# A decoder block on one core: three norms' weights loaded first, the memory's later, seven unread products ahead of them

## The chip, the cores and the metric

The kernel runs on one core of one Trainium2 chip. The metric is device time in microseconds (us) of one execution. TensorE (PE, with its weight loads listed apart as PEld), VectorE (DVE), ScalarE (ACT), GpSimd (POOL) and SyncE (SP) each take their own instructions in a fixed order and wait for each other, and for DMA transfers, through semaphores. ACTq and SPq are DMA issues from the ACT and the SP stream.

## What is computed

One layer (DEPTH is 1) of a decoder block on a 256x2048 input, all in float32. What matters here is its start: the first norm and the first projection.

```
def rmsnorm(x, gain):
    y = xf * lax.rsqrt(jnp.mean(xf * xf, axis=-1, keepdims=True) + NORM_EPS)
    return (y * gain.astype(jnp.float32)).astype(x.dtype)
...
        h = rmsnorm(x, g[0])
        y = hybrid_mixer(h, ...)                       # z = h @ w_in, then attention, gMLP, RWKV-7
        x = x + rmsnorm(y, g[1])
        h = rmsnorm(x, g[2])
        y = memory_cross_attention(h, rmsnorm(mem, mem_src_gain[l]), ...)
        x = x + rmsnorm(y, g[3])
        h = rmsnorm(x, g[4])
        y = conv_ffn(h, ...)
        x = x + rmsnorm(y, g[5])
```

So four weight vectors of 2048 are needed as columns (one value per partition): g[0], g[2], g[4] and `mem_src_gain`. Only g[0] is needed at the start; `mem_src_gain` is used hundreds of microseconds later.

## The kernel before

All matrix products run on TensorE as sums of three products of "hi" and "lo" halves of float32 values. A weight block of 512 KB is loaded into a `raw` buffer (four of them) from the SP stream; ACT casts it to `hi` (L234) and DVE subtracts to get `lo` (L236), three buffers of each. `wstat` (L255) multiplies them with the transposed input: for every 128 rows of weights one product hi x h.hi (L266), one hi x h.lo (L268) and one lo x h.hi (L271), each 128x256.

The input is loaded by eight transfers `x` (L437, names x_76 to x_92 in the listings), and transposed on TensorE in 128x128 pieces (L389) into PSUM tiles `auxp` and `auxq`. ACT multiplies a piece by the norm's weight, a column of `gpar`, and writes the hi half `h` (L375); DVE writes the lo half (L376). There are 16 such pairs. The norm's row factor is applied later: ACT squares x (L408), the sums go over DVE and POOL (L417) to a product with the unit matrix (L424) that lays the factors out along a row, `rrow`.

`gpar` holds the four norms' weights. Before, two transfers from the ACT stream fill the 64 rows of `grow`, one transpose (L469) and one copy (L470) make `gpar` of it:

```
grow = sp.tile([4 * KT, P], F32, name="grow")                                                   # L452
nc.scalar.dma_start(grow[:3 * KT, :], gains[0:6:2].rearrange("g (k p) -> g k p", p=P))          # L454
nc.scalar.dma_start(grow[3 * KT:, :], a["mem_src_gain"][0].rearrange("(k p) -> k p", p=P))      # L455
...
nc.tensor.transpose(ps[:, :4 * KT], grow, ident[:4 * KT, :4 * KT])                              # L469
gcopy = nc.vector.tensor_copy(gpar, ps[:, :4 * KT])                                             # L470
```

`split` makes every `lo` wait to be issued until after `gcopy`. The first projections are a 128-column block (the low-rank inputs, 48 products into one PSUM tile) and then blocks of 256 columns for the RWKV keys (96 products into two tiles). Small tables follow between them: a product `tab` x `oneh` (L531), transposes of `prow` (L512) and of `crow` (L543). When the 128-column block is finished, DVE and ACT make `zl` of it (L607 to L609), and three times a pair of loads `wa` from the ACT stream (L633, L634, one buffer) feeds eight recorded products with `zl` (L642).

The order of each engine's stream is set when the program is built, by a scheduler: it goes by data dependences, by priorities that the code gives (`high_priority` with an offset, `issue_after`), and by the scheduler's own estimate of when things are ready. Each engine then keeps to that order whatever happens on the chip. So a change to a few lines can move instructions of other lines.

Of the kernel before, what the change touches and what calls it, by code (L numbers as in the profile page):

```python
# [12 lines left out]
F32 = mybir.dt.float32  # L13
# [7 lines left out]
P = 128  # L21
D = 2048
S = 256
KT = D // P
# [148 lines left out]
def hybrid_block(tc, a, out, dbg=None):  # L173
    nc = tc.nc
    dbg = dbg or {}
    with ExitStack() as ctx:
# [14 lines left out]
        def mk(pool, tag, bufs, shape=(P, 512), dt=F32):  # L191
            t = pool.tile(list(shape), dt, tag=tag, bufs=bufs, name=nm(tag))
            return t
# [8 lines left out]
        def auxp():  # L202
            return mk(pp, "auxp", 2)

        def auxq():
            return mk(pp, "auxq", 2)
# [11 lines left out]
        def raw_load(src, k0, nk, c0, nco, ahead=AHEAD):  # L218
            if (k0, nk, c0, nco) in early:
                return early.pop((k0, nk, c0, nco))  # L220
            raw = mk(wp, "raw", RAW_BUFS, (P, RAW))
            rv = raw[:, :nk * nco].rearrange("p (k c) -> p k c", k=nk)
            with tc.high_priority(offset=ahead):
                nc.sync.dma_start(rv, src[k0 * P:(k0 + nk) * P, c0:c0 + nco]
                                  .rearrange("(k p) c -> p k c", p=P))
            return rv
# [185 lines left out]
        def factors_of(part):  # L412
# [4 lines left out]
            last_pow[0] = nc.gpsimd.tensor_tensor(r, ss, mhalf[:, :2], op=ALU.pow)  # L417
            return r

        def over_rows(r):  # L420

            ps = auxp()
            for t in range(2):
                nc.tensor.matmul(ps[:, t * P:(t + 1) * P], lhsT=r[:, t:t + 1].to_broadcast([P, P]), rhs=ident,  # L424
                                 start=True, stop=True)
            row = mk(cp, "rrow", 1, (P, S))
            nc.vector.tensor_copy(row, ps[:, :S])
            return row
# [19 lines left out]
        gains = a["sandwich_gains"][0]  # L448
        x2d = a["x"][0]
        start = ExitStack()  # L450
        sp = start.enter_context(tc.tile_pool(name="sp", bufs=1))
        grow = sp.tile([4 * KT, P], F32, name="grow")  # L452
        with tc.high_priority(offset=4 * AHEAD):
            nc.scalar.dma_start(grow[:3 * KT, :], gains[0:6:2].rearrange("g (k p) -> g k p", p=P))  # L454
            nc.scalar.dma_start(grow[3 * KT:, :], a["mem_src_gain"][0].rearrange("(k p) -> k p", p=P))  # L455

            def first_weights():
                early[0, 8, COL_LO, P] = raw_load(a["w_in"][0], 0, 8, COL_LO, P, 0)
            xt = load_rows(x2d, lambda: mk(sp, "x", 8), nc.sync, first_weights)
# [4 lines left out]
        with tc.high_priority(offset=4 * AHEAD):  # L464
            ident = cp.tile([P, P], F32, name="ident")
            make_identity(nc, ident)
            gpar = cp.tile([P, 4 * KT], F32, name="gpar")
            ps = auxp()
            nc.tensor.transpose(ps[:, :4 * KT], grow, ident[:4 * KT, :4 * KT])  # L469
            gcopy = nc.vector.tensor_copy(gpar, ps[:, :4 * KT])  # L470

        def gcol(n):
            return lambda k: gpar[:, n * KT + k:n * KT + k + 1]
# [1 line left out]
        with tc.high_priority(offset=4 * AHEAD):  # L475
            hT = Packed(2)
            pins = []
            for _ in transposed(hT, xt, gcol(0), hbuf):
                pins.append(hT.last)
        rx = row_factors(xt, lambda: mk(sp, "tmp", 4), (None, None, pins[3], pins[5]))  # L480
        xrow = over_rows(rx)


# [17 lines left out]
        for key, src, n in (("mu", a["rwkv_mu"][0], 21), ("w0", a["rwkv_w0"][0], 6),  # L501
                            ("a0", a["rwkv_a0"][0], 6), ("k_k", a["rwkv_k_k"][0], 6),
                            ("k_a", a["rwkv_k_a"][0], 6),
                            ("r_k", a["rwkv_r_k"][0].rearrange("h d -> (h d)"), 6),
                            ("ag", a["attn_out_gain"][0], 6), ("sg", a["sgu_out_gain"][0], 4),
                            ("sb", a["sgu_b"][0].rearrange("g i -> (g i)"), 8)):
            nc.sync.dma_start(prow[r0:r0 + n, :], src.rearrange("(n p) -> n p", p=P))
            off[key] = r0
            r0 += n
        par = cp.tile([P, NPR], F32, name="par")  # L510
        ps = auxp()
        nc.tensor.transpose(ps[:, :NPR], prow[:NPR, :], ident[:NPR, :NPR])  # L512
        nc.vector.tensor_copy(par, ps[:, :NPR])
        omu = cp.tile([P, 21], F32, name="omu")
# [15 lines left out]
        ps = auxp()  # L530
# [10 lines left out]
        ps = auxp()  # L541
# [18 lines left out]
        def colt():  # L560
            return mk(mp, "col", 8)
# [447 lines left out]
        ps = wstat(w_in, COL_LO, P, hT)  # L1009
# [7 lines left out]
        for key, col, mucol, new in (("K", COL_CK, 6, colt), ("R", COL_CR, 0, colt),  # L1017
                                     ("V", COL_CV, 12, lambda: vt()[:, :512])):
            for i in range(3):
                take("v" if key == "V" else "col")  # L1020
                g = new()
                ps = wstat(w_in, col + i * 256, 2 * P, hT)
# [5 lines left out]
        ps = wstat(w_in, COL_LO + P, 2 * P, hT)  # L1028
# [349 lines left out]
        for j in range(2):  # L1378
            ps = wstat(wkv, j * 256, 256, mT)
            k = colt()  # L1380
# [7 lines left out]
        for j in range(2):  # L1388
            ps = wstat(wq, j * 256, 256, h2T)
# [6 lines left out]
        for h in range(4):  # L1396
            qh = qTs[h // 2][:, (h % 2) * S:(h % 2) * S + S]
            kh = kTs[h // 2][:, (h % 2) * S:(h % 2) * S + S]
            ps = auxq()
            for t in range(2):  # L1400
                nc.tensor.matmul(ps[:, t * S:(t + 1) * S], lhsT=qh[:, t * P:(t + 1) * P], rhs=kh,
                                 start=True, stop=True)
# [31 lines left out]
        for h in range(4):  # L1434
            po = auxq()
            for m in range(2):
                nc.tensor.matmul(po[:, :S], lhsT=vm[m][:, h * P:(h + 1) * P], rhs=pTs[h][:, m * S:(m + 1) * S],
                                 start=(m == 0), stop=(m == 1))
# [95 lines left out]
        for j in range(1, FT // 2):  # L1534
            g = mk(fp, "gv", 4)
            ps = wstat2(w_up, j * 256, 256, h3T)
# [6 lines left out]
            ps = wstat2(w_up, D_FF + j * 256, 256, h3T)  # L1543
# [39 lines left out]
```

## Time and profile before

| | |
|---|---|
| runs | 1348.06, 1348.78, 1353.36 us; median 1348.78 |
| profiled execution | 1352.56 us, its span 1350.8 us |
| mean granted TensorE clock in it | 0.992 |
| PE busy | 98% |
| DVE, ACT, POOL busy | 65%, 52%, 11% |

PE is busy nearly throughout; the slices of the page in which it is not are the first and the last. Idle time of the other engines matters only where PE waits for them. The granted clock is given as a share of full speed: 1.00 is 2.4 GHz, 0.50 is 1.2 GHz.

### The profile page before, as it was taken

Reading aid. Unit: us, or ns where it says so; the run is one execution under the profiler, and the core shown is the slowest. Engines: PE = TensorE matmul, PEld = TensorE weight load, DVE = VectorE, ACT = ScalarE, POOL = GpSimd, SP = SyncE. Lnnn points to the kernel's source line nnn. Section 1 sums busy time; section 2 is a strip of 40 time slices with the busy share of each in tenths; the row PEclk is TensorE's granted clock in tenths of the full one; section 3 lists DMA queues with packets and bytes.
Section 4 is the critical chain, followed back from the end, with each engine's and each line's share of the span. In section 5 each row is a group of like instructions: output and inputs, shape, how many; then the busy total and the mean of one; then the engine's idle time right before and its main releaser. Section 6 shows DMA issues by size and latency. Waiting matters only on the chain.

```text
span 1350.8 us, 20948 instructions
## 1 busy us (share of the span) xinstructions
PE 1317.6 (98%) x8184; PEld 1157.1 (86%) x8184; DVE 873.6 (65%) x1300; ACT 708.3 (52%) x1077; POOL 143.9 (11%) x179
## 2 busy tenths in 40 slices
PE   6899999999999999999999999999999999999997
PEld 6789979998987889879888888888888888888886
DVE  5578974466666666566867677776767674445444
ACT  6665363244456655456655555555555553444442
POOL 3010101120014100000111111111111120000000
PEclk9899999999999999999999999999999999999999
DMA  7444553155447755444666666666666666666553
GB/s 226 138 142 142 156 172 111 40 178 165 141 143 271 251 177 187 156 154 129 195 192 189 188 189 191 193 191 188 188 190 191 193 221 193 196 190 196 191 195 133
DMA packets 189841, 238.82 MB, mean 177 GB/s; under 512 B 7920, under 2 KB 144013, under 8 KB 189741
## 3 DMA queue, kind: packets, MB, share of 16 engines
q1 hardware_dynamic: 185514, 225.23, 53.7%
q0 software_dynamic: 3376, 11.29, 2.5%
q8 instruction: 64, 1.05, 0.3%
q10 hardware_dynamic: 851, 0.95, 0.2%
q14 instruction: 36, 0.29, 0.1%
HBM read 235.33 MB, written 2.12 MB: 176 GB/s over the span
## 4 chain that ended last, share of the span: by engine, by line
PE 93%; DVE 2%; issue 1%; DMA 1%; ACT 1%; POOL 1%; ACTq 0%; DVEq 0%; POOLq 0%
PE mm L302 23%; PE mm L304 11%; PE mm L324 11%; PE mm L326 11%; PE mm L330 11%; PE mm L271 6%; PE mm L266 5%; PE mm L268 5%; PE mm L287 2%; DMA wa<-in_rwkv_w_up_dram 1%; PE auxq L678 1%; DVE lo L236 1%; DMA raw<-in_w_in_dram 0%; PE auxp L389 0%; PE auxq L389 0%
## 5 line engine op out<-in xcount | busy, mean ns | idle before, releaser
L236 DVE TENSOR_TENSOR lo<-raw,hi 128x1024 fp32r<-128x1024 f32 x422 | 519.4, 1232 | 368.4 <-ACT hi L234 365.4
L234 ACT CAST hi<-raw 128x1024 fp32r<-128x1024 f32 x422 | 443.4, 1051 | 438.2 <-PE mm L326 169.1
L302 PE MATMUL mm<-h,hi 128*128 128x512 f32 x1344 | 466.2, 394 | 0.0
L304 PE MATMUL mm<-h,lo 128*128 128x256 f32 x1344 | 372.3, 277 | 0.0
L302 PEld LDWEIGHTS mm<-h,hi 128*128 128x128 f32 x1344 | 252.0, 188 | 58.6
L304 PEld LDWEIGHTS mm<-h,lo 128*128 128x128 f32 x1344 | 252.2, 188 | 0.0
L266 PE MATMUL mm<-h,hi 128*128 128x256 f32 x592 | 155.2, 293 | 1.6 <-ACT h L375 1.6
L268 PE MATMUL mm<-h,hi 128*128 128x256 f32 x592 | 152.3, 288 | 0.0
L324 PE MATMUL mm<-hi,hid 128*128 128x512 f32 x352 | 136.9, 389 | 0.0
L326 PE MATMUL mm<-hi,hid 128*128 128x512 f32 x352 | 136.9, 389 | 0.0
L266 PEld LDWEIGHTS mm<-h,hi 128*128 128x128 f32 x592 | 115.6, 196 | 3.9 <-ACT h L375 1.8
L268 PEld LDWEIGHTS mm<-h,hi 128*128 128x128 f32 x592 | 115.4, 195 | 0.4 <-issue 0.3
L1498 POOL TENSOR_TENSOR z<-z,rrow 128x256 f32<-128x256 f32 x84 | 70.2, 836 | 397.3 <-DVE z L1497 397.3
L330 PE MATMUL mm<-lo,hid 128*128 128x512 f32 x352 | 108.3, 389 | 0.0
L271 PE MATMUL mm<-h,lo 128*128 128x256 f32 x592 | 99.1, 289 | 0.0
L271 PEld LDWEIGHTS mm<-h,lo 128*128 128x128 f32 x592 | 84.1, 196 | 1.9 <-issue 1.6
L324 PE MATMUL mm<-hi,h 128*128 128x512 f32 (+1 forms) x208 | 79.2, 386 | 1.7 <-ACT hi L234 1.7
L324 PEld LDWEIGHTS mm<-hi,hid 128*128 128x128 f32 x352 | 66.1, 188 | 13.8
L330 PEld LDWEIGHTS mm<-lo,hid 128*128 128x128 f32 x352 | 66.1, 188 | 13.7
L326 PEld LDWEIGHTS mm<-hi,hid 128*128 128x128 f32 x352 | 66.0, 188 | 13.6
L326 PE MATMUL mm<-hi,h 128*128 128x512 f32 (+1 forms) x208 | 77.0, 375 | 0.0
L330 PE MATMUL mm<-lo,h 128*128 128x512 f32 (+1 forms) x208 | 59.8, 375 | 0.2 <-DVE lo L236 0.2
(352 smaller groups left out, 1547.5 us busy)
## 6 DMA issues: line engine op xcount, KB each, us to landing
raw<-in_ffn_w_up_dram SPq DMA_DIRECT2D x176, 512.0 KB, 4.6
raw<-in_w_in_dram SPq DMA_DIRECT2D x94, 512.0 KB, 4.3
raw<-in_ffn_w_down_dram SPq DMA_DIRECT2D x88, 512.0 KB, 4.9
raw<-in_w_out_dram SPq DMA_DIRECT2D x32, 512.0 KB, 4.6
raw<-in_mem_wkv_dram SPq DMA_DIRECT2D x16, 512.0 KB, 4.0
raw<-in_mem_wq_dram SPq DMA_DIRECT2D x8, 512.0 KB, 3.4
raw<-in_mem_wo_dram SPq DMA_DIRECT2D x8, 512.0 KB, 3.8
x<-in_x_dram SPq DMA_DIRECT2D x8, 256.0 KB, 6.7
```

The source lines that it names most:

```text
L234: nc.scalar.copy(hv, rv)
L236: nc.vector.tensor_tensor(lv, rv, hv.bitcast(F32), op=ALU.subtract)
L266: nc.tensor.matmul(o, lhsT=hv[:, k, cs], rhs=X.h(k0 + k), start=(k0 + k == 0), stop=False)
L268: nc.tensor.matmul(o, lhsT=hv[:, k, cs], rhs=X.l(k0 + k), start=False, stop=False)
L271: L.last = nc.tensor.matmul(o, lhsT=lv[:, k, cs], rhs=X.h(k0 + k), start=False, stop=(k0 + k == nk - 1))
L287: L.last = nc.tensor.matmul(ps[g][t][:, :S], lhsT=w[:, k, cs], rhs=x(k0 + k), start=(k0 + k == 0 and i == 0), stop=(k0 + k == KT - 1 and i ...
L302: nc.tensor.matmul(view(ps[t], z=2, t=S), lhsT=hv[:, k, cs], rhs=X.hl[k0 + k], start=(k0 + k == 0), stop=False)
L304: L.last = nc.tensor.matmul(ps[t][:, S:], lhsT=lv[:, k, cs], rhs=X.h(k0 + k), start=False, stop=(k0 + k == KT - 1))
L324: nc.tensor.matmul(o, lhsT=X.h(kk)[:, ts_], rhs=hv[:, k, :], start=(first and k0 + k == 0), stop=False)
L326: nc.tensor.matmul(o, lhsT=X.l(kk)[:, ts_], rhs=hv[:, k, :], start=False, stop=False)
L330: L.last = nc.tensor.matmul(o, lhsT=X.h(kk)[:, ts_], rhs=lv[:, k, :], start=False, stop=(last and k0 + k == nk - 1))
L1498: nc.gpsimd.tensor_tensor(z, z, got["x2row"], op=ALU.mult)
```

## The change

`grow` keeps the 48 rows of g[0], g[2], g[4] and has one transfer. `mem_src_gain` goes to a tile of its own, loaded from the SP stream behind the nine small `prow` loads, and is transposed and copied next to `prow`. Ahead of the first transpose come seven products of the unit matrix with itself into a PSUM tile that nobody reads, and that transpose is to be issued after the last of them. Nothing of the result is left out. Lines below L424 move by 7 and later by up to 12 in the listings of the change.

```diff
+        def keep_busy(n):
+
+            ps = auxq()
+            for _ in range(n):
+                r = nc.tensor.matmul(ps[:, :P], lhsT=ident, rhs=ident, start=True, stop=True)
+            return r
...
-        grow = sp.tile([4 * KT, P], F32, name="grow")
+        grow = sp.tile([3 * KT, P], F32, name="grow")
+        grow2 = sp.tile([KT, P], F32, name="grow2")
         with tc.high_priority(offset=4 * AHEAD):
-            nc.scalar.dma_start(grow[:3 * KT, :], gains[0:6:2].rearrange("g (k p) -> g k p", p=P))
-            nc.scalar.dma_start(grow[3 * KT:, :], a["mem_src_gain"][0].rearrange("(k p) -> k p", p=P))
+            nc.scalar.dma_start(grow, gains[0:6:2].rearrange("g (k p) -> g k p", p=P))
...
+            r = keep_busy(7)
             ps = auxp()
-            nc.tensor.transpose(ps[:, :4 * KT], grow, ident[:4 * KT, :4 * KT])
-            gcopy = nc.vector.tensor_copy(gpar, ps[:, :4 * KT])
+            with tc.issue_after(r.ins):
+                nc.tensor.transpose(ps[:, :3 * KT], grow, ident[:3 * KT, :3 * KT])
+            gcopy = nc.vector.tensor_copy(gpar[:, :3 * KT], ps[:, :3 * KT])
...
+        nc.sync.dma_start(grow2, a["mem_src_gain"][0].rearrange("(k p) -> k p", p=P))
         par = cp.tile([P, NPR], F32, name="par")
         ps = auxp()
+        nc.tensor.transpose(ps[:, P:P + KT], grow2, ident[:KT, :KT])
+        nc.vector.tensor_copy(gpar[:, 3 * KT:], ps[:, P:P + KT])
```

The scheduler places more than these lines anew. On PE the order differs within the first 600 or so of some 7650 products and is the same from there on, one place near the end apart. Three places show what moves.

PE, in its first thirty or so instructions. L389 are the transposes of x (L389 in both listings), L266 and L268 products of the first weight blocks: `mm_289` (`mm_300` in the change) takes the 128-column block, of which hi_290 (hi_301) is the first half, `mm_365` and `mm_366` take the first 256-column block, of which hi_369 is the first quarter. Ahead of these rows stand, before, the transpose of the norms' weights and that of x_76 and x_78; in the change the seven products of the unit matrix (five, then one behind each of the first two transposes of x), the same transposes, and that of the weights. Before:

```order
L389 MATMUL auxp_129<-ident,x_82 128x128 x2
L389 MATMUL auxp_129<-ident,x_84 128x128 x2
L389 MATMUL auxq_140<-ident,x_82 128x128 x2
L389 MATMUL auxq_140<-ident,x_84 128x128 x2
L266 MATMUL mm_289<-h_112,hi_290 128x256
L389 MATMUL auxp_151<-ident,x_86 128x128 x2
L389 MATMUL auxp_151<-ident,x_88 128x128 x2
L268 MATMUL mm_289<-h_113,hi_290 128x256
L266 MATMUL mm_289<-h_112,hi_290 128x256
L268 MATMUL mm_289<-h_113,hi_290 128x256
L266 MATMUL mm_289<-h_123,hi_290 128x256
L389 MATMUL auxq_162<-ident,x_86 128x128 x2
```

and of the change:

```order
L389 MATMUL auxq_148<-ident,x_82 128x128 x2
L389 MATMUL auxq_148<-ident,x_84 128x128 x2
L266 MATMUL mm_300<-h_120,hi_301 128x256
L266 MATMUL mm_365<-h_120,hi_369 128x256
L266 MATMUL mm_366<-h_120,hi_369 128x256
L268 MATMUL mm_300<-h_121,hi_301 128x256
L268 MATMUL mm_365<-h_121,hi_369 128x256
L268 MATMUL mm_366<-h_121,hi_369 128x256
L266 MATMUL mm_300<-h_120,hi_301 128x256
L266 MATMUL mm_365<-h_120,hi_369 128x256
L266 MATMUL mm_366<-h_120,hi_369 128x256
L389 MATMUL auxp_159<-ident,x_86 128x128 x2
```

The products with hi_369, the third weight block to be loaded, now stand ahead of the transposes of x_86 to x_92; before, only products with the first block do.

ACT, around the first casts (L234) and the first writes of `h` (L375). raw_80, raw_318 (raw_329 in the change) and raw_356 (raw_367) are the first, second and third weight block to be loaded, in both listings. Before:

```order
L408 ACTIVATE tmp_200,rpart_195<-x_82 128x512
L408 ACTIVATE tmp_202,rpart_195<-x_84 128x512
L375 ACTIVATE h_112<-auxp_107,gpar 128x256
L375 ACTIVATE h_123<-auxq_118,gpar 128x256
L375 ACTIVATE h_112<-auxp_107,gpar 128x256
L375 ACTIVATE h_134<-auxp_129,gpar 128x256
L375 ACTIVATE h_123<-auxq_118,gpar 128x256
L375 ACTIVATE h_145<-auxq_140,gpar 128x256
L375 ACTIVATE h_134<-auxp_129,gpar 128x256
L375 ACTIVATE h_156<-auxp_151,gpar 128x256
L234 CAST hi_320<-raw_318 128x1024
```

and of the change:

```order
L408 ACTIVATE tmp_210,rpart_203<-x_84 128x512
L234 CAST hi_331<-raw_329 128x1024
L375 ACTIVATE h_120<-auxp_115,gpar 128x256
L234 CAST hi_369<-raw_367 128x1024
L375 ACTIVATE h_131<-auxq_126,gpar 128x256
L375 ACTIVATE h_120<-auxp_115,gpar 128x256
L375 ACTIVATE h_142<-auxp_137,gpar 128x256
L375 ACTIVATE h_153<-auxq_148,gpar 128x256
L375 ACTIVATE h_131<-auxq_126,gpar 128x256
```

Before, eight writes of `h` stand ahead of the cast of the second block; now that cast is ahead of all of them, and the cast of the third block ahead of all but one.

PE, around the first products with `zl` (L642 before, L654 in the change). `mm_543` and `mm_553` belong to the second 256-column block, `mm_366` to the first. Before:

```order
L268 MATMUL mm_543<-h_124,hi_546 128x256
L271 MATMUL mm_543<-h_112,lo_547 128x256 x2
L271 MATMUL mm_543<-h_123,lo_547 128x256
L642 MATMUL auxp_380<-zl,wa_374 128x256
L642 MATMUL auxp_381<-zl,wa_374 128x256
L642 MATMUL auxp_380<-zl,wa_374 128x256
L642 MATMUL auxp_381<-zl,wa_374 128x256
L271 MATMUL mm_543<-h_123,lo_547 128x256
L266 MATMUL mm_543<-h_134,hi_585 128x256
```

and of the change:

```order
L268 MATMUL mm_366<-h_198,hi_507 128x256
L271 MATMUL mm_366<-h_186,lo_508 128x256 x2
L271 MATMUL mm_366<-h_197,lo_508 128x256
L654 MATMUL auxp_391<-zl,wa_385 128x256
L654 MATMUL auxp_392<-zl,wa_385 128x256
L654 MATMUL auxp_391<-zl,wa_385 128x256
L654 MATMUL auxp_392<-zl,wa_385 128x256
L271 MATMUL mm_366<-h_197,lo_508 128x256
L266 MATMUL mm_553<-h_120,hi_557 128x256
L268 MATMUL mm_553<-h_121,hi_557 128x256
L266 MATMUL mm_553<-h_120,hi_557 128x256
```

In the change the first products with `zl` stand at the end of the first 256-column block; before, 38 products of the second block stand between that end and them. Between the first and the second set of products with `zl` there are 28 products of 128x256 in the change and 38 before; between the second and the third 56 in the change. The product L531 (L543 in the change) stood in the middle of the fourth quarter of the first 256-column block; it now stands in the middle of its second, 61 products ahead of the first with `zl`.

## Rows read from the trace of the kernel before

**Rows 1.** The page's first part: busy time, share of the span and number of instructions of each engine.

```profile
span 1350.8 us, 20948 instructions
PE 1317.6 (98%) x8184; PEld 1157.1 (86%) x8184; DVE 873.6 (65%) x1300; ACT 708.3 (52%) x1077; POOL 143.9 (11%) x179
```

**Rows 2.** Who waited for whom, PE, over the whole span: line, what ended the wait, us in total, times, longest.

```profile
PE auxp L469 <- DMA grow<-in_mem_src_gain_dram: 7.9, 1, 7.9
...
PE auxp L531 <- issue: 2.2, 1, 2.2
...
PE auxp L642 <- DMA wa<-in_rwkv_w_up_dram: 1.3, 1, 1.3
```

**Rows 3.** The timeline of the first 12 us: start, duration, engine, line, operation, what it writes and reads, how many merged, and in brackets the idle time of the engine before and what ended it.

```profile
0.81 1.38 ACTq L454 DMA_DIRECT2D grow<-in_sandwich_gains_dram  x1
...
1.31 0.29 POOL masks.py:199 TENSOR_SCALAR_AFFINE_SELECT ident<-ident 128x128 f32<-128x128 f32 x1
...
5.69 0.48 ACTq L634 DMA_DIRECT2D wa<-in_rwkv_a_up_dram  x1
...
7.89 0.34 PE L469 MATMUL auxp<-ident,grow 64*128 64x64 f32 x1 [7.89 <-DMA grow<-in_mem_src_gain_dram]
...
8.16 1.11 PE L389 MATMUL auxp<-ident,x 128*128 128x128 f32 x4
8.27 0.23 DVE L470 COPY gpar<-auxp 128x64 f32<-128x64 f32 x1 [6.28 <-PE auxp L469]
...
9.19 4.61 SPq L224 DMA_DIRECT2D raw<-in_w_in_dram  x4
...
10.18 0.46 ACT L375 ACTIVATE h<-auxp,gpar 128x256 fp32r<-128x256 f32 x1
...
11.19 0.84 ACT L375 ACTIVATE h<-auxp,gpar 128x256 fp32r<-128x256 f32 x2 [0.19 <-DVE h L376]
```

**Rows 4.** Five stretches: their length, then busy time and number of instructions of PE, PEld, DVE, ACT, POOL, the granted TensorE clock, the busy share of the DMA engines and what they moved in GB/s.

```profile
4.00:8.00 4.00, 0.11 (x1) 0.14 (x1) 0.00 (x0) 2.02 (x6) 0.00 (x0) 1.00 1.00 302
...
14.00:18.00 4.00, 1.88 (x14) 1.47 (x13) 1.48 (x3) 2.42 (x5) 0.00 (x0) 1.00 1.10 349
20.00:22.50 2.50, 2.50 (x14) 2.50 (x14) 2.37 (x5) 2.50 (x7) 0.00 (x0) 0.50 0.75 233
24.00:28.00 4.00, 4.00 (x36) 4.00 (x35) 1.41 (x3) 2.00 (x2) 4.00 (x3) 1.00 0.42 129
37.00:43.00 6.00, 6.00 (x25) 4.78 (x24) 1.28 (x2) 1.04 (x1) 0.55 (x1) 0.50 0.43 122
```

**Rows 5.** The timelines of PE and of ACT from 13 to 26 us.

```profile
13.38 0.60 PE L389 MATMUL auxq<-ident,x 128*128 128x128 f32 x4
...
20.35 0.41 PE L266 MATMUL mm<-h,hi 128*128 128x256 f32 x1
20.56 0.41 PE L268 MATMUL mm<-h,hi 128*128 128x256 f32 x1
...
25.05 0.28 PE L266 MATMUL mm<-h,hi 128*128 128x256 f32 x1
25.17 0.28 PE L268 MATMUL mm<-h,hi 128*128 128x256 f32 x1
...
25.65 0.60 PE L424 MATMUL auxp<-ident,rs 128*128 128x128 f32 x4
...
15.59 1.04 ACT L234 CAST hi<-raw 128x1024 fp32r<-128x1024 f32 x1 [2.00 <-DMA raw<-in_w_in_dram]
...
22.16 0.66 ACT L408 ACTIVATE tmp<-x 128x512 f32<-128x512 f32 x1
...
23.39 0.50 ACT L375 ACTIVATE h<-auxq,gpar 128x256 fp32r<-128x256 f32 x1
```

**Rows 6.** The timelines of SP, POOL and PE from 28 to 42 us.

```profile
28.68 1.52 SPq L224 DMA_DIRECT2D raw<-in_w_in_dram  x2
30.25 0.49 SPq L527 DMA_DIRECT2D oneh<-in_c_onehot_dram  x1
29.89 0.75 POOL L616 DMA_DIRECT2D lg<-in_rwkv_ln_gain_dram  x1
...
36.86 1.43 PE L531 MATMUL auxp<-oneh,tab 32*12 32x384 f32 x2 [2.22 <-issue]
...
41.80 0.41 PE L266 MATMUL mm<-h,hi 128*128 128x256 f32 x1
```

**Rows 7.** The timelines of PE and of ACT from 47 to 65 us, the three sets of products with `zl` and the loads `wa` of the second and third.

```profile
47.88 1.13 PE L642 MATMUL auxp<-zl,wa 64*128 64x256 f32 x8 [0.31 <-ACT zl L1011]
...
55.06 1.55 PE L642 MATMUL auxp<-zl,wa 64*128 64x256 f32 x8 [1.31 <-DMA wa<-in_rwkv_w_up_dram]
...
57.20 1.06 PE L271 MATMUL mm<-h,lo 128*128 128x256 f32 x4
...
64.09 1.14 PE L642 MATMUL auxp<-zl,wa 64*128 64x256 f32 x8
...
50.95 0.48 ACTq L633 DMA_DIRECT2D wa<-in_rwkv_w_up_dram  x1
...
60.06 0.47 ACTq L633 DMA_DIRECT2D wa<-in_rwkv_w_up_dram  x1
```

## The prediction, as put on record before the changed kernel ran

> **What bounds the kernel now.** Start with the page's busy times [rows 1]: PE works 98% of 1350.8 us. So time can only come from PE's few idle stretches and from stretches at the lower clock, and everything that PE loses or wins in the start is carried unchanged to the end, because the order behind the first 600 products is the same. The second view is PE's waits [rows 2]: the longest is the first, 7.9 us, put down to the load of the memory norm's weights; 2.2 us before the table product L531 and 1.3 us before a product with `zl` are the others that the change touches. The third is the timeline of the start [rows 3], read for what comes right behind that first wait: the transposes begin at 8.16, `gpar` is copied at 8.27, the first `h` is written at 10.18. The fourth is the table of stretches [rows 4]. The DMA engines are busy 1.00 of the stretch from 4 to 8 us and 1.10 of that from 14 to 18, at 302 and 349 GB/s: the first 18 us are a stretch that the transfers fill. And the second weight block is cast only at 15.59, after 2.00 us in which ACT waited for that block's transfer [rows 5]. That is the release to remember.
>
> **The wait that is removed.** The load that is left on ACT's queue is issued from 0.81 to 2.19; it had landed when L634, which waits for its semaphore, was issued at 5.69 [rows 3]. The memory's 8 KB held the transpose until 7.89. So the weights can be transposed at 5.7, and `gpar` is there some 2.2 us earlier. The 8 KB move to SP behind the small tables, where nothing near waits for them, and their transpose and copy are one short instruction on PE and on DVE (0.34 and 0.23 for the whole 64 rows [rows 3]).
>
> **The seven products.** Two of the existing products with the unit matrix are four recorded instructions in 0.60 us [rows 5]; the slow transposes at 8.16 take 1.11 us for four [rows 3]. So seven cost between 2.1 and 3.9 us. The unit matrix is ready at 1.60 [rows 3], so they run in time that PE waits through anyway. Cost on the path: 0.
>
> **What the new order moves.** The listing has the cast of the second block ahead of all 16 writes of `h`, where eight were ahead of it, and the third block's cast ahead of all but one. The second block's bytes stand behind x and the first block as before, in a stretch where the DMA engines are full, and its issue, at 9.19 [rows 3], waits for the load of `wa`, as it did. So I take its landing as unchanged, 15.59. ACT then stands still from about 10 to 15.6 with eight writes of `h` behind it, and PE, with 16 of 32 transposes done, stands too. From 15.59 ACT has 16 writes at 0.84 for two minus the overlap, 0.38 each [rows 3], 4 squares at 0.66 and 4 casts at 1.05 [rows 5]: 6.1 + 2.6 + 4.2 = 12.9 us. The same count for before (8 writes, 4 squares, 3 casts) gives 8.8, ending 24.4, and the trace has 23.89 [rows 5]; less that 0.5 the last `h` comes at 28.0 instead of 23.9.
>
> **What of that reaches PE.** I count to one point: the end of the 144 products of the first two column blocks. Before, the next block's first product starts at 41.80 [rows 6]. In the change 66 of the 144 stand ahead of the last `h`, and 78 behind. At 0.12 us from start to start at the full clock [rows 5] these take 9.4 us, the row factors, the table product and the transposes of `crow` about 1.9 more. From 28.4 that ends at 39.7, if nothing waits. But the table product now comes after 16 of those products, at about 31, and it needs `oneh`, whose issue waits behind a weight block for a buffer: that buffer is free when DVE has subtracted the fourth block, whose cast stands behind 13 writes, 2 squares and 2 casts and so ends near 25.0; with DVE's share of the writes in between I put the release at 27.5 and the issue at 28. Before it took 6.6 us from issue (30.25) to product (36.86), with two weight blocks and a 384 KB load in front of it [rows 6]; with one block in front I take 4.5 to 6.5, so PE waits until 32.5 to 34.5, 1.5 to 3.5 us, where it waited 2.2. That puts the point at 41.2 to 43.2. Then the clock: behind the wait before L531 it is 0.50 from 37 to 43 [rows 4], 0.21 from start to start instead of 0.12 [rows 5], 24 products by 0.09 or 2.2 us. Whether a wait of 1.5 to 3.5 us brings it down again I leave half open and take 1.1. The transposes of `crow`, some 0.45, were behind the point before. Sum at the point: 42.2 + 1.1 - 0.45 = 42.8 against 41.8, **+1.0**; ends -1.1 (short wait, full clock) and +3.1.
>
> **The loads for the products with `zl`.** The first set frees `wa`, ACT works on it, and only then is the next pair loaded: from the first set to the second 7.18 us, from the second to the third 9.03 [rows 7], the loads landing 4.0 us after their issues at 50.95 and 60.06. That chain is not shortened. What covers it is products between the sets: 38 before, 28 now. 28 by 0.12 and 1.1 for the set leave 2.7 us of 7.18 uncovered, where 1.31 was: +1.4. Between second and third, 56 by 0.12 and 1.3 leave 1.0, where PE did not wait: +1.0. Together **+2.4**; ends 0, if ACT's new order shortens the chain as much, and +3.5, with a clock that falls after them as in the products after 57.20 [rows 7].
>
> **Sum.** 0 + 0 + 1.0 + 2.4 = +3.4 us. The profiled execution took 1352.56 us and would take 1356.0; it lies 3.8 above the median of the runs shown, 1348.78, from which the forecast is 1352.2. All low ends together give 1347.7, all high ends 1355.4. About 0.5%, or 6.7 us, is what a measurement of this kernel can tell from no change, and the forecast is inside it.
>
> **Rivals.** *The clock falls at every wait (slower).* PE waits 3.5 us at the table product and the clock is 0.50 behind it, as in the row from 37 to 43: +3.1. Then it falls behind the second and the third set of products with `zl`; 16 products at 0.09 and 0.4 for the set are 1.9 us, which before is paid once [rows 7]. 3.1 + 2.4 + 1.9 = +7.4, 1356.2. It decides when each of these waits reaches about 2 us. For it: 2.22 us were enough before L531. Against it: the third set's wait is only 1.0 by my count. 0.14.
>
> *The early start holds (faster).* If the second block landed by about 10 us, nothing would hold ACT, all `h` would come 2.2 us earlier, and the 16 first transposes would run at 0.60 for four instead of 1.11 [rows 3, 5], 2.0 us less: -4.2, 1344.6. The Trainium skill, "TensorE: Matmul & The Clock Gate", Part 1, says that the throttled state is the default and that activity releases it, so products ahead of the real work should give it the full clock; by that rule alone the sum would be 2.0 us lower. Against this rival: in the rows the slow transposes were done 5 us before the block landed at 15.59, and the idle stretch of 5 us that I expect between would leave PE at the lower level again: before, the clock was 0.50 from 20 on, after PE had been busy for 1.88 us of the 4.00 from 14 to 18 [rows 4]. 0.07.
>
> *Only the place of the wait changes (same).* The transfers set the pace, the table load lands early (-1.1) and ACT's chain for `wa` is 1 us shorter in the new order (+1.4): 1349.1. For it: the DMA share of 1.00 and 1.10 [rows 4]. 0.24.
>
> **Chances and range.** Forecast 0.55, the rivals 0.14, 0.07, 0.24. The range takes in the third rival and most of the first and leaves out the second: 1346.5 to 1356.8. Faster by over 0.5% (under 1342.0) needs more than any case gives: 0.02. Slower by over 0.5% (over 1355.5) is the first rival and little else: 0.13. Within: 0.85.
>
> **What would show it.** In the changed profile: the transpose of the weights before 6.5 us, `gpar` copied near 6.5; ACT idle before its second cast, for about 5 us, released by the load of a weight block near 15.6, and the first write of `h` after that cast, at about 16.6; PE idle from about 10 to 17; the last `h` near 28; the first weight product of the third column block 0 to 3 us later than 41.8, or the 144 products ended there; two waits for `wa`, the first near 2.7 us. If the first `h` is written near 8 us, the step on the order fails, and the time should be below 1347. If the wait before the table product is gone, my second step is wrong by up to 2 us the other way. A slow stretch behind 110 us, where the order is the same, would be something that I have not seen.

## The result, and the profile of the changed kernel

Before: median 1349.07 us (1346.53 to 1353.36). After: **1353.63 us** (1349.63 to 1356.43), 20 runs each. The ratio is 1.0027 with a 95% interval of 1.0018 to 1.0036, so the change costs 2.4 to 4.9 us: a small loss, within the 0.5% that the prediction called no change, and near the forecast of 1352.2.

The two profiles hide it. The execution profiled after took 1353.09 us (span 1351.4), close to its median; the one before took 1352.56 (span 1350.8), 3.5 above its own. They differ by 0.6 where the medians differ by 4.6. So a second execution of the kernel before was profiled (first experiment), and what is said below of before is checked against both.

The page's first part, beside [rows 1]:

```profile
span 1351.4 us, 20985 instructions
PE 1321.6 (98%) x8199; PEld 1158.6 (86%) x8199; DVE 871.5 (64%) x1301; ACT 708.6 (52%) x1077; POOL 144.3 (11%) x179
```

PE is busy 4.0 us longer. The seven products alone are busy for 3.8 us (14 recorded instructions, at 1.2 GHz), so they account for nearly all of it. PE's waits over the whole span, beside [rows 2] (line, what ended the wait, us in total, times, longest):

```profile
PE mm L266 <- ACT h L375: 4.5, 1, 4.5
...
PE auxq L424 <- POOL ident masks.py:199: 1.7, 1, 1.7
PE auxp L654 <- DMA wa<-in_rwkv_a_up_dram: 1.6, 1, 1.6
...
PE auxp L654 <- DMA wa<-in_rwkv_w_up_dram: 0.7, 1, 0.7
```

The wait of 7.9 us for the memory's weights is gone, and so is the one before the table product. In their place stands one of 4.5 us for ACT's first `h`, and 2.3 instead of 1.3 us for `wa`. The timeline of ACT (start, duration, operation, in brackets the idle time and what ended it) says why, beside [rows 5]:

```profile
10.68 0.19 ACT L408 ACTIVATION_READ_ACCUMULATOR tmp<-x 128x1 f32 x1
14.73 1.04 ACT L234 CAST hi<-raw 128x1024 fp32r<-128x1024 f32 x1 [3.86 <-DMA raw<-in_w_in_dram]
15.68 0.47 ACT L375 ACTIVATE h<-auxp,gpar 128x256 fp32r<-128x256 f32 x1
...
23.59 0.47 ACT L375 ACTIVATE h<-auxq,gpar 128x256 fp32r<-128x256 f32 x1 [1.99 <-PE auxq L389]
...
29.53 0.47 ACT L375 ACTIVATE h<-auxq,gpar 128x256 fp32r<-128x256 f32 x1
```

ACT has the second block's cast at the head of its queue and stands still for 3.86 us until that block lands; the first `h` comes at 15.68 (10.18 before), the last at 29.53 (23.39). One row is new to me: at 23.59 ACT waits 1.99 us for a transpose on PE. PE's timeline, beside [rows 3, 5, 6, 7]:

```profile
1.65 2.50 PE L424 MATMUL auxq<-ident 128*128 128x128 f32 x10 [1.65 <-POOL ident masks.py:199]
...
6.63 0.34 PE L478 MATMUL auxp<-ident,grow 48*128 48x48 f32 x1
6.91 1.11 PE L389 MATMUL auxp<-ident,x 128*128 128x128 f32 x4
...
16.20 0.58 PE L266 MATMUL mm<-h,hi 128*128 128x256 f32 x1 [4.49 <-ACT h L375]
...
22.17 0.41 PE L268 MATMUL mm<-h,hi 128*128 128x256 f32 x1
22.38 0.41 PE L266 MATMUL mm<-h,hi 128*128 128x256 f32 x1
...
24.62 0.28 PE L266 MATMUL mm<-h,hi 128*128 128x256 f32 x1
24.74 0.28 PE L268 MATMUL mm<-h,hi 128*128 128x256 f32 x1
...
33.26 0.81 PE L543 MATMUL auxp<-oneh,tab 32*12 32x384 f32 x2
...
41.94 1.14 PE L654 MATMUL auxp<-zl,wa 64*128 64x256 f32 x8
43.23 0.28 PE L266 MATMUL mm<-h,hi 128*128 128x256 f32 x1
...
47.27 1.10 PE L654 MATMUL auxp<-zl,wa 64*128 64x256 f32 x4 [0.66 <-DMA wa<-in_rwkv_w_up_dram]
50.01 1.43 PE L654 MATMUL auxp<-zl,wa 64*128 64x256 f32 x4 [1.64 <-DMA wa<-in_rwkv_a_up_dram]
...
59.45 1.14 PE L654 MATMUL auxp<-zl,wa 64*128 64x256 f32 x8
```

Behind the 4.5 us of waiting PE runs at 1.2 GHz until about 23.4 (products 0.21 us from start to start), then at 2.4 (0.12). The point of the prediction, the end of the 144 products, is 43.23 less the set of `zl` products that now stands ahead of it (1.07): 42.16, against 41.80 [rows 6].

**A marker for all runs.** The first product that reads `center` and `v` (L867 before, L879 here) starts near 137 us in both, behind all that is reordered but for one place near the end; from it to the span's end every execution in the table below has 1213.2 to 1216.0 us. What PE did up to it splits a run's loss into waiting and slow work. The row for after (stretch, then busy us and instructions of PE, PEld, DVE, ACT, POOL, granted clock, DMA share, GB/s):

```profile
0.00:137.31 137.31, 123.81 (x947) 116.16 (x948) 92.40 (x160) 81.86 (x127) 18.20 (x26) 0.99 0.56 163
```

137.31 less 123.81 is 13.50 us of waiting. The same row for the others:

| kernel | marker | PE busy | PE waits | last `h` | median, us | ratio to before (95%) |
|---|---|---|---|---|---|---|
| before, first profile | 137.08 | 120.22 | 16.86 | 23.39 | 1349.07 | |
| before, again | 134.82 | 119.22 | 15.60 | 23.35 | 1349.70 | 0.9996 (0.9980-1.0011) |
| after | 137.31 | 123.81 | 13.50 | 29.53 | 1353.63 | 1.0027 (1.0018-1.0036) |
| products only | 138.51 | 122.83 | 15.68 | 29.84 | 1354.13 | 1.0030 (1.0018-1.0042) |
| split only | 131.92 | 119.00 | 12.92 | 22.93 | 1349.34 | 0.9994 (0.9982-1.0006) |
| casts ahead, no products | 138.02 | 116.35 | 21.67 | 28.40 | 1352.84 | 1.0036 (1.0021-1.0051) |
| casts held behind | 128.99 | 121.01 | 7.98 | 23.25 | 1344.65 | 0.9966 (0.9952-0.9980) |
| three products | 136.28 | 121.43 | 14.85 | 26.89 | 1350.75 | 1.0013 (0.9998-1.0027) |
| five products | 135.86 | 121.93 | 13.93 | 27.17 | 1351.62 | 1.0013 (1.0000-1.0026) |
| idle time filled, 10 | 135.87 | 124.71 | 11.16 | 27.21 | 1352.74 | 1.0025 (1.0012-1.0037) |
| idle time filled, 16 | | | | | 1354.38 | 1.0041 (1.0029-1.0054) |
| table early | 133.34 | 117.61 | 15.73 | 22.85 | 1349.42 | 1.0005 (0.9993-1.0017) |
| two buffers for `wa` | 142.15 | 126.91 | 15.24 | 30.22 | 1357.90 | 1.0062 (1.0046-1.0079) |
| held, two for `wa` | 138.58 | 128.01 | 10.57 | 24.34 | 1354.61 | 1.0035 (1.0018-1.0052) |

Each ratio is to runs of before on the same chip (their medians 1348.45 to 1349.42). Marker, busy, waits and last `h` are of one execution each. Of the version with sixteen filling products one execution of seven ran throughout at a granted clock of 0.556 and took 2188 us; it is not in the median and the ratio.

### The profile page after: what moved, and what is told of

It reads as the page before. It is cut to its first block, busy times and chain, and to the rows that moved or that the text cites. A ratio compares the mean times of both kernels' runs of the same rounds, so it can differ in the third digit from the quotient of the medians.

```text
span 1351.4 us, 20985 instructions
## 1 busy us (share of the span) xinstructions
PE 1321.6 (98%) x8199; PEld 1158.6 (86%) x8199; DVE 871.5 (64%) x1301; ACT 708.6 (52%) x1077; POOL 144.3 (11%) x179
## 4 chain that ended last, share of the span: by engine, by line
PE 91%; DVE 4%; issue 1%; DMA 1%; ACT 1%; POOL 1%; ACTq 0%; POOLq 0%; DVEq 0%
PE mm L302 23%; PE mm L304 11%; PE mm L324 11%; PE mm L330 11%; PE mm L326 10%; PE mm L266 5%; PE mm L268 5%; PE mm L271 5%; PE mm L287 2%; DVE lo L236 1%; DMA wa<-in_rwkv_a_up_dram 1%; PE auxq L690 1%; ACT hi L234 1%; PE auxp L389 1%; DMA raw<-in_w_in_dram 0%
## 5 line engine op out<-in xcount | busy, mean ns | idle before, releaser
L234 ACT CAST hi<-raw 128x1024 fp32r<-128x1024 f32 x422 | 443.2, 1051 | 433.8 <-PE mm L326 169.0
L266 PE MATMUL mm<-h,hi 128*128 128x256 f32 x592 | 154.0, 292 | 5.0 <-ACT h L375 4.5
L268 PE MATMUL mm<-h,hi 128*128 128x256 f32 x592 | 151.6, 288 | 0.0
L266 PEld LDWEIGHTS mm<-h,hi 128*128 128x128 f32 x592 | 114.8, 195 | 7.6 <-ACT h L375 4.9
L268 PEld LDWEIGHTS mm<-h,hi 128*128 128x128 f32 x592 | 114.8, 195 | 0.8 <-issue 0.6
```

Of the source, the lines that this page charges most:

```text
L234: nc.scalar.copy(hv, rv)
L266: nc.tensor.matmul(o, lhsT=hv[:, k, cs], rhs=X.h(k0 + k), start=(k0 + k == 0), stop=False)
L268: nc.tensor.matmul(o, lhsT=hv[:, k, cs], rhs=X.l(k0 + k), start=False, stop=False)
```

## The experiments

**The kernel before, again.** No edit.

> The kernel before, unchanged, for a second profiled execution and a second set of times. The profiled execution shown with it was 3.8 us above the median of its runs, while the changed kernel's was 0.5 below its own, so the two profiles differ by 0.6 us of span where the medians differ by 4.6. Theory 1 (the order costs the time): median 1348 to 1350; if this profile is a short execution (near 1347.5), it is shorter than the first one in the first 65 us: the wait of 2.2 us at the table product, or the clock of 1.2 GHz behind it (36.9 to 43.2 us), is shorter or gone. Rival (the difference lies at the end, in the last transfers): the first 140 us are as before and 3 to 5 us differ behind 1,340 us.

Measured: 1349.70, this execution with a span of 1348.3. The first theory holds as far as it goes, the rival fell. The same product that starts at 41.80 in the first profile [rows 6] starts at 39.16 here, and from the marker on the two agree within 0.3 us:

```profile
35.64 0.80 PE L531 MATMUL auxp<-oneh,tab 32*12 32x384 f32 x2 [1.83 <-issue]
36.37 0.75 PE L271 MATMUL mm<-h,lo 128*128 128x256 f32 x4
...
37.19 0.28 PE L266 MATMUL mm<-h,hi 128*128 128x256 f32 x1
...
39.16 0.41 PE L266 MATMUL mm<-h,hi 128*128 128x256 f32 x1
```

The wait is nearly the same, 1.83 against 2.22; the table product behind it takes 0.80 instead of 1.43, and the slow products begin only about 37.5. Of the 2.64 us, 1.22 are there already when the table product starts (35.64 against 36.86), and 1.42 come from there to this product (3.52 against 4.94). Where the clock falls behind a wait differs from execution to execution, and that is much of why one program's times here spread over 7 us and more. Against this execution the changed kernel is 3.0 us later at the point and 2.5 at the marker, which is at the low end of the measured 2.4 to 4.9.

**Products only.** Before with `keep_busy(7)`, `grow` still one tile of four norms:

```diff
...
+            r = keep_busy(7)
             ps = auxp()
-            nc.tensor.transpose(ps[:, :4 * KT], grow, ident[:4 * KT, :4 * KT])
+            with tc.issue_after(r.ins):
+                nc.tensor.transpose(ps[:, :4 * KT], grow, ident[:4 * KT, :4 * KT])
```

> Only the seven unread products before the transpose of the weights; the memory's weights still load and transpose with the others. ScalarE's order is that of the changed kernel (the casts of the second and third block ahead of nearly all h writes). Theory 1 (the order, which the products bring about, costs the time): as the changed kernel, 1352 to 1355, ScalarE idle from about 11 to 14.7 us and last h near 29.5. Rival A (the split of the weights, with the later transpose of the memory's and the earlier loads of wa, costs it): 1348.5 to 1350, as before.

Measured: 1354.13, the whole loss. ACT waits for the second block until 16.13 here, and the last `h` comes at 29.84:

```profile
16.13 1.04 ACT L234 CAST hi<-raw 128x1024 fp32r<-128x1024 f32 x1 [5.66 <-DMA raw<-in_w_in_dram]
```

**Split only.** The changed kernel without `keep_busy` and the `issue_after` on it.

> Only the split of the weights: three norms' first, the memory's later behind the parameter rows; no products. ScalarE's order in the first 50 instructions is that of the kernel before. Theory 1 (the order costs the time): 1347.5 to 1350, last h near 23.5 us, and the weights' copy about 1 to 2 us earlier, which the wait for the second block hides. Rival A (the split costs it): 1352 to 1355.

Measured: 1349.34, as before. The weights are there earlier and it is worth nothing that can be measured. Rival A fell.

**Casts ahead, without products.** Is the order enough by itself? In the kernel before, three blocks are split ahead of the `h` writes, and the writes wait for those casts:

```diff
...
-            for _ in transposed(hT, xt, gcol(0), hbuf):
+            for k0, n, c0, nco in ((0, 8, COL_LO, P), (8, 8, COL_LO, P), (0, 4, COL_LO + P, 256)):
+                with tc.issue_after(last_x[0].ins) if cast else ExitStack():
+                    rv = raw_load(a["w_in"][0], k0, n, c0, nco, 0)
+                ready[k0, n, c0, nco] = split(rv, n, nco)
+            for _ in transposed(hT, xt, gcol(0), hbuf, hold=lambda k: cast[min(k, 1) + 1]):
```

> The kernel before, without products and with all weights together, but the casts of the second and third block written ahead of the h writes, so that ScalarE's order is that of the changed kernel. Theory 1 (the order alone costs the time): 1351 to 1354.5, ScalarE idle until the second block lands, first h at 15.5 to 17 us, last h at 28 to 30. Rival (the products cost something of their own, which the pinned kernel hid by other gains): 1348 to 1350, as before.

Measured: 1352.84, 1.0036 times before: the whole loss again, with no product and no split in it. The two waits of PE at the start, and ACT's timeline:

```profile
PE auxp L477 <- DMA grow<-in_mem_src_gain_dram: 7.9, 1, 7.9
PE mm L273 <- ACT h L382: 5.6, 1, 5.6
```

```profile
16.05 1.04 ACT L236 CAST hi<-raw 128x1024 fp32r<-128x1024 f32 x1 [5.52 <-DMA raw<-in_w_in_dram]
17.00 0.47 ACT L382 ACTIVATE h<-auxp,gpar 128x256 fp32r<-128x256 f32 x1
```

**Casts held behind.** And is it needed? The changed kernel, products and split included, with three casts held behind `h` writes (`pins`):

```diff
+        casts = [0]
+        behind = {1: 2, 2: 3, 3: 4}
...
-                nc.scalar.copy(hv, rv)
+                n = behind.get(casts[0])
+                casts[0] += 1
+                with tc.issue_after(pins[n].ins) if n is not None else ExitStack():
+                    nc.scalar.copy(hv, rv)
```

> The changed kernel with products and split, but the casts of the second, third and fourth block held behind the h writes of the third, fourth and fifth pair, so that ScalarE's order is about that of the kernel before. Theory 1 (the order costs the time): 1347 to 1350, first h near 8 to 11 us instead of 15.7, last h near 24. Rival B (the products themselves cost it, by TensorE's time or its clock): still 1352 to 1355.

Measured: **1344.65**, 0.9966 times before and 9 us under the changed kernel: lower than I expected, and the one version that beats both. Rival B fell: the same products, and no loss. Its rows, ACT and then PE up to the marker:

```profile
11.26 0.46 ACT L381 ACTIVATE h<-auxp,gpar 128x256 fp32r<-128x256 f32 x1
...
14.94 1.05 ACT L240 CAST hi<-raw 128x1024 fp32r<-128x1024 f32 x1 [1.03 <-DMA raw<-in_w_in_dram]
```

```profile
0.00:128.99 128.99, 121.01 (x948) 114.10 (x949) 91.75 (x160) 81.12 (x127) 17.98 (x26) 1.00 0.60 173
```

Against after, PE waits 5.5 us less and its work takes 2.8 less: the wait for `h`, and the slow clock. PE's order moves with ACT's: between the transposes the changed kernel has products by threes (from 17.31 us on), the held version single ones. But casts ahead has single ones too, and the loss, all of it as waiting (21.67 us up to the marker, against 16.86 and 15.60); so ACT's order is enough. What makes this version better than before is not settled either. The hold without the products was not run: in split only 8, 11 and 13 writes of `h` already stand ahead of the three casts, where the hold asks for 6, 8 and 10, so I expect it to change nothing. Against split only 4.9 us of waiting are gone: 3.5 in the first 12 us (no gain: PE works 3.5 us more there, and the products are busy for 3.8), 1.0 from 12 to 24, the table's wait of 1.9, 0.6 from 72 to 84, with 1.2 more from 24 to 36 and 1.1 more from 48 to 60. Beside the products, that leaves 1.4 us less of waiting and some 1.8 less of work at the marker. The products and the hold make another order together, and which of its places gives the gain was not tried.

**Three and five products.** `keep_busy(3)`, `keep_busy(5)` in the changed kernel.

> The changed kernel with three unread products instead of seven: in ScalarE's order six h writes stand ahead of the second block's cast (none with seven, eight without products). Theory 1 (the order costs the time, the products nothing): 1344.5 to 1349, first h near 11, last h near 24. Rival B (the products cost it): in proportion to three of seven, 1350.5 to 1352.

> The changed kernel with five unread products: one h write stands ahead of the second block's cast, two ahead of the third's. Theory 1: between, since one h write alone lets TensorE begin early but the next products wait for the cast: 1349 to 1353, with the first h near 11 and a wait of 2 to 4 us behind the first products. If the position of the casts matters only where no h is ahead: 1345 to 1349.

Measured: 1350.75 and 1351.62. Five is inside its range. Three misses Theory 1's range and lies in rival B's, which the two experiments above exclude. Its trace shows what my count of `h` writes left out:

```profile
16.59 1.04 ACT L234 CAST hi<-raw 128x1024 fp32r<-128x1024 f32 x1 [2.88 <-DMA raw<-in_w_in_dram]
```

```profile
18.06 0.49 PE L266 MATMUL mm<-h,hi 128*128 128x256 f32 x1 [2.22 <-ACT h L375]
```

Six writes were ahead of the cast; in the held version seven, and there the block landed at 14.94, here at 16.59. PE waited 2.2 us for just that seventh write, and ran slow from 19.4 to 25. The landing of that block differs from profile to profile, 14.30 to 16.59; an order that has `h` writes behind it that PE needs soon pays for every late one. How much of this run's loss is the missing write and how much the late block is not separated.

**Idle time filled.** The changed kernel, with 16 and then 10 more unread products behind the fourth pair's transposes:

```diff
-                        nc.tensor.transpose(pv[:, k, t * P:(t + 1) * P],
+                        X.last_t = nc.tensor.transpose(pv[:, k, t * P:(t + 1) * P],
...
+                if len(pins) == 4:
+                    fill = mmps()
+                    with tc.issue_after(hT.last_t.ins):
+                        for _ in range(16):
+                            nc.tensor.matmul(fill[:, :P], lhsT=ident, rhs=ident, start=True, stop=True)
```

> The changed kernel with 16 more unread products of the unit matrix between the transposes and the first product of x, so that TensorE works through the 4.5 us (11.7 to 16.2) in which it waits for ScalarE's first h write; ScalarE's order is the same. If what the wait costs is the wait and the clock of 1.2 GHz behind it (17.3 to 23.3 us, products 0.21 us apart instead of 0.12), the second part goes: half of 6 us, 2.5 to 3 us, so 1350.5 to 1351.5, with the products 0.12 apart from about 17 us. If the clock there has another cause, or what follows waits for ScalarE anyway (last h at 29.5): 1353 to 1354.5, as the changed kernel.

> The changed kernel with ten more unread products in the 4.5 us (11.7 to 16.2) in which TensorE waits for the first h write; with sixteen they ran on to 18.1 us, past the wait, and the time was 1354.4. Ten take about 4.2 us and end near 15.8. If the clock of 1.2 GHz behind the wait (17.3 to 23.3 us) is a cost of its own: 2.5 to 3 us less than the changed kernel, 1350.5 to 1351.5, with products 0.12 us apart from about 17 us. If what follows waits for ScalarE's h writes anyway: 1352.5 to 1354.5.

Measured: sixteen 1354.38, ratio 1.0041 (1.0029 to 1.0054). The one trace of it is that of the execution of 2188 us. There the fill runs to 18.1 us, past the first `h` at 15.59:

```profile
11.47 6.63 PE L493 MATMUL mm<-ident 128*128 128x128 f32 x32
```

How long it ran in the six timed executions isn't shown. In the trace of ten the products speed up on the way; at 0.11 us an instruction twelve more would end near 15.8, an estimate. So sixteen may have been of the right size there, and their times show no gain. Ten:

```profile
6.38 0.66 PE L389 MATMUL auxp<-ident,x 128*128 128x128 f32 x4
...
10.02 0.69 PE L389 MATMUL auxp<-ident,x 128*128 128x128 f32 x2 [0.88 <-DMA x<-in_x_dram]
...
11.35 3.17 PE L493 MATMUL mm<-ident 128*128 128x128 f32 x20
15.77 0.38 PE L266 MATMUL mm<-h,hi 128*128 128x256 f32 x1 [1.25 <-ACT h L375]
...
19.56 0.28 PE L266 MATMUL mm<-h,hi 128*128 128x256 f32 x1
19.68 0.28 PE L268 MATMUL mm<-h,hi 128*128 128x256 f32 x1
...
40.80 0.28 PE L266 MATMUL mm<-h,hi 128*128 128x256 f32 x1
...
47.03 1.97 PE L659 MATMUL auxp<-zl,wa 64*128 64x256 f32 x4 [0.89 <-DMA wa<-in_rwkv_a_up_dram]
...
53.57 0.41 PE L266 MATMUL mm<-h,hi 128*128 128x256 f32 x1
```

The products from 17 us on are 0.12 apart, as the first theory said, the last `h` comes 2.3 us earlier (27.21) and the point 2.4 (40.80 against 43.23). About 0.4 of this is the second block, which landed at 14.30 here against 14.73; from the first `h` to the last it is 11.96 us against 13.85. So up to the point the slow clock behind the wait is a cost of its own in these traces: slow transposes hold up ACT, which holds up PE. But the time is that of the second theory: at the end only 0.9 is left (1352.74 against 1353.63, not measured side by side; the intervals of the two ratios overlap), and a gain is not shown. Behind the wait for `wa` the slow stretch now lasts from 47.0 to 53.8 instead of about 50.5 to 54.0, and 1.4 us remain at the marker; between 195 and 295 us this execution then loses them again, to 0.8 us more of waiting and a slow stretch (marker to end 1216.0, after 1214.1).

**Table early.** In the kernel before, `tab` and `oneh` are loaded at high priority:

```diff
...
-        nc.sync.dma_start(oneh, a["c_onehot"])
+        with tc.high_priority(offset=4 * AHEAD):
+            nc.sync.dma_start(oneh, a["c_onehot"])
```

> The kernel before with the loads of the bias table and its one-hot matrix issued behind the loads of x instead of between the later blocks; all else nearly as before. Theory (in the kernel before, the 1.8 to 2.2 us of waiting at the table's product and the slow products behind it lie on the path, and the changed kernel is rid of them only because its TensorE comes there late): 1345.5 to 1347.5, no wait at the table's product, clock near 1.00 from 24 to 48 us. Rival (TensorE catches up in the stretch to 130 us, where other chains set the end): 1348.5 to 1350, as before.

Measured: 1349.42, no change. But it doesn't say what the wait cost, because the wait only moved: `lnc`, loaded late as ever, now held the PSUM buffer that the transposes of `crow` need:

```profile
PE auxp L545 <- DVE lnc L534: 1.6, 1, 1.6
```

**Two buffers for `wa`.** In the changed kernel, and in the one with the casts held:

```diff
-                wa = mk(rp, "wa", 1, (P, 256))
+                wa = s1() if i == 1 else mk(rp, "wa", 1, (P, 256))
```

> The changed kernel with a second buffer for wa, so that the second pair of these weights loads at the start. Theory (the waits of 0.7 and 1.6 us at the second set of zl products, and the clock of 1.2 GHz behind them from 51.4 to 53.9 us, lie on the path): 2.3 plus about 1.2 us less, 1350 to 1351.5. Rival (the chains over VectorE, ScalarE and GpSimd at 70 to 97 us set the end anyway): 1353 to 1354.5, as the changed kernel.

> The changed kernel with the casts held behind the h writes and a second buffer for wa. The pinned one was at 1344.7 and has one wait of 1.6 us at the zl products, for ScalarE (oc), not for wa. If wa is no longer what ends it there: 1344 to 1345.5, as pinned; if the first load of the second pair still delays ScalarE's work: 1342.5 to 1344.

Measured: 1357.90 and 1354.61, each worse than without the edit, by 4.3 and 10.0 us (not side by side, but the intervals of the ratios lie apart). Not every execution pays it: one of the six took 1351.64, two of the eight 1348.41 and 1348.46. All theories fell. The waits for `wa` are gone, but the second set moves up close behind the first, and there PE waits for ACT to read the first set's sums out of PSUM (the first of the two, whose start has the slow stretch of the changed kernel too):

```profile
6.32 0.66 PE L389 MATMUL auxp<-ident,x 128*128 128x128 f32 x4
...
22.37 0.41 PE L266 MATMUL mm<-h,hi 128*128 128x256 f32 x1
...
46.11 2.67 PE L654 MATMUL auxp<-zl,s 64*128 64x256 f32 x8 [1.57 <-ACT oc L659]
48.72 0.58 PE L266 MATMUL mm<-h,hi 128*128 128x256 f32 x1
...
60.31 0.41 PE L266 MATMUL mm<-h,hi 128*128 128x256 f32 x1
60.52 0.35 PE L268 MATMUL mm<-h,hi 128*128 128x256 f32 x1
```

Behind a wait of 1.57 us PE works at 1.2 GHz for 14 us, to 60.5; in the held one it is as long, behind 1.86. In the changed kernel it is some 3.5 behind 1.64. What sets that length is open.

## Why the prediction came out as it did

Its main cause, the late `h`, was right, and its size near: +3.4 forecast, +2.4 to +4.9 measured. That the size is near is in part luck: the point cost more than its +1.0, and of the +2.4 for the loads nothing is left at the marker. By its steps:

- **The wait removed, and the products: nothing on the path.** Right. `gpar` was copied at 7.01, 1.3 us earlier and not 2.2 (a transpose of x stands ahead of it now), and split only shows that it is worth nothing. The products run from 1.65 to 5.98 in time that PE waits anyway; casts ahead has the whole loss without them.
- **The new order.** Right, and now shown from both sides: with the order alone the loss comes, with the casts held it goes. The block landed at 14.73 (15.59 taken), the first `h` came at 15.68 (16.6), the last at 29.53 (28.0). From the landing to the last `h` it took 14.8 us where I had 12.4: I let ACT run without a wait and PE at full clock, but the slow transposes held ACT up by 1.99 at 23.59.
- **The point: +1.0.** It was +0.4 against the profile that I counted from and +3.0 against the second one. The parts were off in opposite directions. The wait at the table product, 1.5 to 3.5 by my count, was 0: the product came at 33.26, and `oneh`, issued at 28.43, was there within 4.8 us. That is the "up to 2 us the other way" of my last paragraph. The late `h` was worth more. And I had taken the slow stretch behind L531, 2.2 us, as a property of the kernel; in the second execution the way from L531 to the point is 1.42 us shorter.
- **The loads for `zl`: +2.4.** Half right. At the second set the waits were 0.66 and 1.64, together 2.30 (2.7 forecast, 1.31 before). At the third there was none where I had 1.0: between the sets lay slow products too, and they cover more. And from the point to the marker the changed kernel takes 95.15 us, against 95.28 and 95.66 in the two executions of before: the second of these waited 1.7 us for `wa`, and behind that wait too PE ran slow. So nothing of the +2.4 is left at the marker.
- **The rivals.** The clock did not fall at every wait: the table's was gone, and the stretch behind the second set was some 3.5 us. The early start did not come: the second block landed at 14.73, and in no profile of this study before 14.30. That only the place of the wait changes, 1349.1, lies under the measured interval, which begins at 1351.5. The early start cites the Trainium skill's "TensorE: Matmul & The Clock Gate", Part 1, that activity releases the throttled state. Here the transposes right behind the seven products, at 6.91, still took 1.11 us for four. In two other executions with the same products they took 0.66 (6.38 with idle time filled, 6.32 with two buffers), and by 10.02 and 9.92 the clock was low again. The ten products that end just ahead of the work did help: in that trace the products behind the wait are 0.12 apart, where two buffers, with nearly the same start and no fill, has 0.21 until about 22.9. So the rule agrees with these traces; what it needed was to be applied to the stretch right before the work, and this change puts its products ten microseconds earlier.
- **Behind 110 us** nothing new: from the marker on 1214.1, and 1213.5 and 1213.7 before.

What stays open: how much of the 4.4 us by which the held version beats the kernel before belongs to the products; what the table's wait cost; and what ends a slow stretch.

## What to carry to other kernels

Where a scheduler orders the queues, the cost of an added instruction is first what it does to the order: seven products with a price of zero moved one cast to the head of a queue, where it waited for a transfer with eight ready writes behind it. Compare the order of every engine before the durations, and pin the one instruction that must not go ahead. And before a term is taken from one profile, look at where that execution stands among its runs: two executions of the same program were 2.6 us apart at one product, 1.4 of them behind one wait.

## What the runs showed of the hardware

- The slow stretch behind a wait has no fixed price. Behind waits of 0.66 and 1.64 us (after), of 0.85 and 0.89 (idle time filled, 10) and of 1.57 (two buffers), with the same kinds of products, PE worked at 1.2 GHz for about 3.5, 7 and 14 us. With 2.3 us of waiting for `wa` removed the median rose by 4.3 us.
- The granted clock of a row can miss it: after, it reads 1.00 from 20 to 22.5 us, where products start 0.21 us apart. The distance between starts is the safer reading.

```profile
20.00:22.50 2.50, 2.50 (x14) 2.50 (x13) 1.69 (x5) 1.61 (x5) 0.00 (x0) 1.00 0.71 211
```
